# Four inner RMS norms without TensorE: sums by VectorE's 32x32 turns, the root as a power on GpSimd

## The chip, the cores and the metric

The kernel runs on one core of a Trainium2 chip. A core has TensorE (matrix products), VectorE, ScalarE and GpSimd (elementwise work of three kinds), SyncE (which here only issues loads), and 16 DMA engines. The engines run in parallel, each works through its own instructions in order, and they wait for one another by semaphores. The metric is the device time of the whole kernel in microseconds (us); weights and activations start in the chip's memory (HBM) and the output ends there.

## The reference

A decoder trunk of two layers on 256 tokens of width 1024, everything float32:

```python
def rms_norm(x, g):
    y = x * lax.rsqrt(jnp.mean(x * x, axis=-1, keepdims=True) + EPS)
    return y * g

# layer 0: x += short_conv_mixer(rms_norm(x, a_norm)); x += conv_glu_ffn(rms_norm(x, f_norm[0]))
# shared K, V from rms_norm(x, kv_norm)
# layer 1: x += moba_attention(rms_norm(x, b_norm), K, V); x += conv_glu_ffn(rms_norm(x, f_norm[1]))
# output: rms_norm(x, final_norm)

def short_conv_mixer(h, w_in, conv_w, w_out):      # w_in 1024 x 3072, conv of width 3 over tokens
    b_gate, c_gate, hx = jnp.split(h @ w_in, 3, axis=-1)
    return (b_gate * causal_dwconv(c_gate * hx, conv_w)) @ w_out

def conv_glu_ffn(h, w_up, conv_w, conv_b, w_down): # w_up 1024 x 5632, w_down 2816 x 1024
    u = causal_dwconv(h @ w_up, conv_w) + conv_b
    g, v = jnp.split(u, 2, axis=-1)
    return (jax.nn.silu(g) * v) @ w_down
```

The attention has 16 heads of 64; with 256 tokens there is one block, so it is plain causal attention with a relative position bias. K/V and the queries use the same normalized x up to their gains, so the trunk has five norms with a different sum: the mixer's, the first ConvGLU's, the one of K/V and attention, the second ConvGLU's, and the final one. The first four are called the inner norms.

## The kernel before, in words

**Layout.** Activations are kept transposed: feature on the 128 partitions, 8 tiles (k = 0 to 7) of 256 tokens along the free axis. A weight matrix is cut into units of 128 output columns: a unit "B" is 128x2048 (two groups of 128 columns, 48 matmuls of 128x256), a unit "S" is 128x1024 (24 matmuls). Each product is made of three matmuls on split operands: weight and activation are each split into a high part and a low remainder, and `mm3` (L168) issues high by high, high weight by low activation, low weight by high activation.

**Preparing a weight unit.** SyncE loads it (`rawB`, `rawS`, three buffers each), ScalarE copies it to `hi` (L91), VectorE subtracts to get `lo` (L97). The functions `hi(tag, part, parts)` and `lo(tag, part, parts)` (L102, L109) do this for the next unit in line, whole or a part of it; `lo` also issues the load of the unit three ahead. A unit's matmuls can start when its `hi` is there and need its `lo` at their third step.

**The order of the work.** The schedule is manual: each engine runs its instructions in the order in which the program emits them, and the program sprinkles `hi` and `lo` between the other work by hand. TensorE works through the units one after the other; VectorE and ScalarE prepare later units and do the elementwise work of earlier ones.

**A norm, before.** The matmuls don't wait for the norm. They run on x times the gain; the token's factor 1/rms is multiplied into the products afterwards (`u<-up,rr`, L456 in the mixer, L551 in the ConvGLUs), so `rr`, a tile that holds the 256 factors on every partition, is first wanted there. `boundary` (L304) adds the previous block's products to x, makes the high and low parts of the scaled x (ScalarE, VectorE), and the squares. `sum_squares` (L293) adds the eight squared tiles to one, in two halves. What is left is a sum over the 128 partitions for each token, and it must come back on every partition:

- `rstd_cols` (L338): four matmul records with a vector of ones give the sums as two columns of 128 tokens each (tokens on partitions); VectorE takes the inverse root by a bit trick and three Newton steps (`rsqrt`, L325, 10 small instructions), and scales the identity matrix by it, as high and low part.
- `rstd_rows` (L361 is its matmul): two matmuls of a matrix of ones (`each`) with these diagonal matrices broadcast the factors to all partitions, and ScalarE copies them to `rr` (L364).

TensorE gets these matmuls in the middle of up units whose own matmuls are ready; the mixer's and the ConvGLUs' code therefore splits units 1 and 2 and puts their k = 0 step later. The `again` tiles: `tile_0_again` (L277) makes a copy of activation tile 0 (high by ScalarE, low by VectorE), and a step with `again=True` reads that copy at k = 0. For V and K/V the copy's low part is `va[1]`.

**Around the four places.**
- Mixer: units MC[1], MB[1], MC[2] surround the norm; the first product that needs `rr` is L456, behind ScalarE's square of `rr`. The bias table of the attention (`bias_table`, GpSimd and others) is emitted before the mixer.
- ConvGLU (`ffn`): for unit i the chain is product with `rr` (L551, VectorE), conv (ScalarE L558, VectorE L397), Silu, product, then split parts for the down unit. `conv(i)` also emits the `hi` and `lo` of later units. ScalarE loads the Silu table (L594) with a dummy instruction, `first`, while TensorE does the norm's sum.
- K/V: units v0, v1, v2, then the query/key units; `v_step(1)` (L655 to L658) reads tile 0 in its sixth step, after the norm's sum. The V outputs need the factors as columns (`ycol`), the queries as rows scaled by -1/8 in reversed order.

The final norm (L948 on) already takes its root by a GpSimd power (L961) of one column.

Of the kernel before, what the change touches and what calls it, by code (L numbers as in the profile page):

```python
# [17 lines left out]
S = 256  # L18
# [19 lines left out]
def f32(ap):  # L38
    return ap.bitcast(F32)
# [3 lines left out]
def yoco_kernel(ctx: ExitStack, tc: tile.TileContext, t: dict, out: bass.AP):  # L43
# [95 lines left out]
    each = const.tile([128, 192], F32R, name="each")[:, 48:176]  # L139
# [5 lines left out]
    A.activation(each, ones, AF.Copy)  # L145
# [158 lines left out]
    def boundary(acc, x, gain, order=same, again=True):  # L304
# [11 lines left out]
        lo("B", 0, 2)  # L316
        if not again:
            lo("B", 1, 2)
        sum_squares(sq, 1, order)
        if again:  # L320
            lo("B", 1, 2)
            tile_0_again(xh, xl)
        return xh, xl, sq

    def rsqrt(ms, y, a, eng=V):  # L325

        eng.tensor_scalar(y.bitcast(I32), ms.bitcast(I32), -0.5, float(0x5F3759DF), op0=OP.mult, op1=OP.add)
        for _ in range(3):
            eng.tensor_mul(a, y, y)
            if eng is V:  # L330
                V.scalar_tensor_tensor(a, a, -0.5, ms, op0=OP.mult, op1=OP.mult)
                V.scalar_tensor_tensor(y, a, 1.5, y, op0=OP.add, op1=OP.mult)
            else:
                eng.tensor_mul(a, a, ms)
                eng.tensor_scalar(a, a, -0.5, 1.5, op0=OP.mult, op1=OP.add)
                eng.tensor_mul(y, a, y)

    def rstd_cols(sq, meanwhile=None):  # L338

        ps = psum.tile([128, 512], F32, name="misc", bufs=1)  # L340
        for c in range(2):
            PE.matmul(ps[:, c:c + 1], sq[:, 2, c * 128:(c + 1) * 128], ones[:, 0:1],
                      start=(c == 0), stop=True, skip_group_check=True)
        w = tmp.tile([128, 8], F32, name="nw")
        ms, y, a = w[:, 0:2], w[:, 2:4], w[:, 4:6]
        V.tensor_scalar(ms, ps[:, 0:2], 1.0 / D, EPS, op0=OP.mult, op1=OP.add)
        rsqrt(ms, y, a)
        if meanwhile:
            meanwhile()
        dh, dl = (tmp.tile([128, 384 + 64], F32R, name="d" + x, tag="z" + x, bufs=4)[:, 16:16 + S] for x in "hl")  # L350
        for c in range(2):
            d = slice(c * 128, c * 128 + 128)
            V.tensor_scalar(dh[:, d], ident, y[:, c:c + 1], None, op0=OP.mult)
            V.scalar_tensor_tensor(dl[:, d], ident, y[:, c:c + 1], f32(dh[:, d]), op0=OP.mult, op1=OP.subtract)
        return y, (dh, dl)

    def rstd_rows(dg, scales=(1.0,), orders=(same,)):

        ps = psum.tile([128, 512], F32, name="misc", bufs=1)
        for n in range(2):  # L360
            PE.matmul(ps[:, :S], each, dg[n], start=(n == 0), stop=(n == 1), skip_group_check=True)  # L361
        r = act.tile([128, 2, S], F32, name="rr", bufs=1)
        for n, s in enumerate(scales):
            A.activation(r[:, n, :], orders[n](ps[:, :S]), AF.Copy, scale=s)  # L364
        return r
# [34 lines left out]
    ext = bias_table()  # L400


# [37 lines left out]
    for q in range(4):  # L440
        hi("B", q, 4)
        squares(xT, sq, q)
        lo("B", q, 4)
        if q == 2:
            sum_squares(sq, 0)
    sum_squares(sq, 1)
    tile_0_again(xh, xl)
# [30 lines left out]
    up_step(MC[1], mc[1], xh, xl, 2, range(1, 8), first=1)  # L478
    MC[1].used = False

    def quarter(q):
# [61 lines left out]
    def ffn(layer, xh, xl, sq, bank=down_bank, between=None):  # L543
# [40 lines left out]
        for i in range(FJ):  # L584
            if between and i >= 20:
                between(i - 4, acc)
            if i != 2:
                ub[i] = up_bank()
# [461 lines left out]
```

## Time and profile before

| | before |
|---|---|
| runs | 567.91, 567.95, 567.37 us |
| median | 567.91 us |
| profiled execution | 567.37 us, its span 565.6 us |
| granted TensorE clock, mean | 0.998 |
| TensorE / VectorE / ScalarE / GpSimd busy | 559.0 / 473.5 / 341.4 / 9.6 us |

The span is the time from the first to the last profiled instruction; the execution's own time is a little longer. In a row of the trace the columns are: start in us from the span's start, duration in us, engine (PE = TensorE, DVE = VectorE, ACT = ScalarE, POOL = GpSimd), line of the kernel, operation, output<-inputs, shape and type of output and inputs, count, and in brackets, where it is given, the idle time before it on its engine with what ended it. A row of the view of groups has, after the count, total busy us and mean ns of one, then idle before it. A row of the view of stretches has the stretch, its length, TensorE's busy time with its count of matmuls in brackets, its busy share, the DMA share and GB/s moved.

### The profile page before, as it was taken

How to read it: one execution, taken by the hardware profiler on the slowest of the kernel's cores; microseconds unless marked ns; L12 is line 12 of the kernel's file. 1: busy time of each engine (PE TensorE's matmuls, PEld its weight loads, DVE VectorE, ACT ScalarE, POOL GpSimd, SP SyncE). 2: the span in 40 equal slices, each digit the busy share in tenths (PEclk: the TensorE clock that was granted, in tenths of full speed). 3: DMA queues.
4: the chain of work that ended last, by engine and by line, in shares of the span. 5: the costliest groups of instructions: out<-in, count | busy, mean ns of one | idle time of the engine just before them, and what ended most of it. 6: DMA issues, size and time to landing. Idle time of an engine off the chain costs nothing.

```text
span 565.6 us, 11835 instructions
## 1 busy us (share of the span) xinstructions
PE 559.0 (99%) x4908; PEld 555.4 (98%) x4908; DVE 473.5 (84%) x823; ACT 341.4 (60%) x528; POOL 9.6 (2%) x29
## 2 busy tenths in 40 slices
PE   9999999999999999999999999999999999999996
PEld 9999999999999999999999999999999999999995
DVE  6998869899877787787897999858999898889885
ACT  7765437567654565466756777656676566556444
POOL 0400000000000000000000000000000000000001
PEclk9999999999999999999999999999999999999999
DMA  8986573446556545655255555554656654553211
GB/s 292 387 303 223 192 294 113 159 147 247 194 189 224 189 161 209 224 177 196 76 212 169 192 216 219 191 184 150 224 187 220 226 184 165 213 222 114 75 38 75
DMA packets 24181, 108.48 MB, mean 192 GB/s; under 512 B 2736, under 2 KB 5440, under 8 KB 16192
## 3 DMA queue, kind: packets, MB, share of 16 engines
q1 hardware_dynamic: 23840, 107.43, 53.2%
q8 instruction: 38, 0.62, 0.5%
q10 hardware_dynamic: 288, 0.30, 0.1%
q14 instruction: 15, 0.12, 0.1%
HBM read 106.65 MB, written 1.07 MB: 190 GB/s over the span
## 4 chain that ended last, share of the span: by engine, by line
PE 98%; issue 0%; DVE 0%; ACT 0%; POOL 0%; POOLq 0%
PE up L169 20%; PE up L170 19%; PE up L171 19%; PE acc L169 7%; PE acc L170 7%; PE acc L171 7%; PE acc L202 3%; PE acc L203 3%; PE acc L200 3%; PE up L413 1%; PE up L785 1%; PE acc L655 1%; PE acc L657 1%; PE acc L658 1%; PE misc L142 1%; PE acc L710 1%
## 5 line engine op out<-in xcount | busy, mean ns | idle before, releaser
L169 PE MATMUL up<-xh,hiB 128*128 128x256 f32 x928 | 256.9, 277 | 0.0
L171 PE MATMUL up<-xh,loB 128*128 128x256 f32 x928 | 256.4, 276 | 0.0
L170 PE MATMUL up<-xl,hiB 128*128 128x256 f32 x928 | 256.3, 276 | 0.0
L169 PEld LDWEIGHTS up<-xh,hiB 128*128 128x128 f32 x928 | 174.2, 188 | 0.5 <-issue 0.3
L170 PEld LDWEIGHTS up<-xl,hiB 128*128 128x128 f32 x928 | 174.3, 188 | 0.0
L171 PEld LDWEIGHTS up<-xh,loB 128*128 128x128 f32 x928 | 174.2, 188 | 0.0
L97 DVE TENSOR_TENSOR loB<-rawB,hiB 128x2048 fp32r<-128x2048 f32 (+3 forms) x78 | 147.9, 1901 | 3.7 <-ACT hiB L91 3.5
L91 ACT ACTIVATE hiB<-rawB 128x2048 fp32r<-128x2048 f32 (+2 forms) x75 | 123.8, 1656 | 14.7 <-PE up L170 7.0
L558 ACT ACTIVATE cv<-u,pk 128x256 f32<-128x256 f32 x88 | 48.2, 595 | 69.3 <-DVE u L551 69.3
L97 DVE TENSOR_TENSOR loS<-rawS,hiS 128x1024 fp32r<-128x1024 f32 (+2 forms) x73 | 83.5, 1147 | 7.1 <-ACT hiS L91 6.8
L397 DVE SCALAR_TENSOR_TENSOR cv<-u,pk,cv 128x255 f32<-128x255 f32 x192 | 81.4, 479 | 2.7 <-ACT cv L558 1.7
L91 ACT ACTIVATE hiS<-rawS 128x1024 fp32r<-128x1024 f32 (+2 forms) x73 | 72.0, 987 | 8.9 <-PE acc L170 5.3
L171 PE MATMUL acc<-sh,loS 128*128 128x256 f32 x240 | 66.2, 276 | 0.0
L169 PE MATMUL acc<-sh,hiS 128*128 128x256 f32 x240 | 66.2, 276 | 0.0
L170 PE MATMUL acc<-sl,hiS 128*128 128x256 f32 x240 | 66.2, 276 | 0.0
L551 DVE TENSOR_TENSOR u<-up,rr 128x512 f32<-128x512 f32 x44 | 30.3, 689 | 42.5 <-PE up L171 40.6
L394 ACT ACTIVATE sh<-hid 128x256 fp32r<-128x256 f32 x52 | 21.7, 417 | 58.5 <-DVE hid L575 53.7
L170 PEld LDWEIGHTS acc<-sl,hiS 128*128 128x128 f32 x240 | 45.1, 188 | 0.0
L171 PEld LDWEIGHTS acc<-sh,loS 128*128 128x128 f32 x240 | 45.0, 188 | 0.0
L169 PEld LDWEIGHTS acc<-sh,hiS 128*128 128x128 f32 x240 | 45.0, 188 | 0.0
L200 PE MATMUL acc<-hiS,sh 128*128 128x256 f32 x154 | 42.5, 276 | 0.0
L202 PE MATMUL acc<-loS,sh 128*128 128x256 f32 x154 | 42.5, 276 | 0.0
(196 smaller groups left out, 796.0 us busy)
## 6 DMA issues: line engine op xcount, KB each, us to landing
rawB<-w_up SPq DMA_DIRECT2D x44, 1024.0 KB, 4.7
rawS<-w_dn SPq DMA_DIRECT2D x44, 512.0 KB, 3.4
rawB<-w_qk SPq DMA_DIRECT2D x8, 1024.0 KB, 4.8
rawB<-w_mc SPq DMA_DIRECT2D x6, 1024.0 KB, 7.6
rawS<-w_mo SPq DMA_DIRECT2D x8, 512.0 KB, 4.8
rawB<-w_v SPq DMA_DIRECT2D x4, 1024.0 KB, 4.8
rawS<-w_o SPq DMA_DIRECT2D x8, 512.0 KB, 4.0
rawS<-w_mb SPq DMA_DIRECT2D x7, 512.0 KB, 5.3
```

The costliest lines, as they stand in the source:

```text
L91: A.activation(self.hi[:, c], self.raw[:, c], AF.Copy)
L97: V.tensor_sub(self.lo[:, c], self.raw[:, c], f32(self.hi[:, c]))
L169: PE.matmul(o, wh, xh, start=start, stop=False, skip_group_check=True)
L170: PE.matmul(o, wh, xl, start=False, stop=False, skip_group_check=True)
L171: PE.matmul(o, wl, xh, start=False, stop=stop, skip_group_check=True)
L200: PE.matmul(o, hh[:, tok], u.hi[:, f], start=(first and (apart or d.start == 0)), stop=False, skip_group_check=True)
L202: PE.matmul(o, hh[:, tok], u.lo[:, f], start=False, stop=False, skip_group_check=True)
L203: PE.matmul(o, hl[:, tok], u.hi[:, f], start=False, stop=last, skip_group_check=True)
L394: return (h, lw), lambda: A.activation(h, src, AF.Copy), lambda: V.tensor_sub(lw, src, f32(h))
L397: V.scalar_tensor_tensor(o[:, back:], u[:, :S - back], w, o[:, back:], op0=OP.mult, op1=OP.add)
L551: V.tensor_mul(u, ub[j], rr[:, 0:1, :].to_broadcast([128, 2, S]))
L558: A.activation(o[:, half, :], u[:, half, :], AF.Identity, scale=cw[half][2], bias=par(P_FCB, c0 + half * FJ))
```

## The change

The sums over partitions, the inverse roots and the broadcast leave TensorE. Three new functions do them:

- `roots`: VectorE transposes the summed squares (128 x 256) in blocks of 32x32 (`V.transpose`) into a free part of the same tile, and reduces each block along its free axis: 8 columns on 128 partitions. Partition 32a+j now holds, in column b, the sum over the 32 rows of block row a of the token 32b+j. ScalarE makes three copies from partition groups 1 to 3 ("quadrants") to group 0; VectorE adds the four, scales by 1/D and adds EPS; GpSimd raises to the power -0.5; ScalarE copies the result from group 0 to the other three groups. Two callbacks, `early` and `late`, emit work meanwhile: low weights in three places, low activations for the queries in K/V.
- `rows`: one VectorE transpose of the factors, each read 32 times with a stride of zero, gives `rr` on all partitions.
- `root_rows` allocates `rr`.

`rsqrt`, `rstd_cols`, `rstd_rows` and the matrix `each` with its ScalarE copy at the start are gone. With no norm matmuls, units MC[1], MB[1], MC[2], MC[3], the ConvGLUs' units and the V and query units run whole, in the usual order of k but for the mixer's MC[1]; reads of the copied tile 0 are gone except in MC[1], v1, v3 and q0. `boundary` emits the whole low B unit ahead of the second half of the sums, for all three callers, and no copy of tile 0. In the mixer the bias table is emitted behind `roots`; `ext` is the table's tile.

```diff
-    each = const.tile([128, 192], F32R, name="each")[:, 48:176]
+    sums = const.tile([128, 64], F32, name="sums")
+    ycol = const.tile([128, 64], F32, name="ycol")
+    halves = const.tile([128, 64], F32, name="halves")
+    G.memset(halves, -0.5)
...
-    A.activation(each, ones, AF.Copy)
...
         sum_squares(sq, 0)
-        lo("B", 0, 2)
-        if not again:
-            lo("B", 1, 2)
+        lo("B")
         sum_squares(sq, 1, order)
-        if again:
-            lo("B", 1, 2)
-            tile_0_again(xh, xl)
         return xh, xl, sq
...
+    def roots(sq, early, late):
+
+        y = tmp.tile([128, 8], F32, name="nw")
+        t = sq[:, 3, :]
+        V.transpose(t, sq[:, 2, :])
+        V.tensor_reduce(sums[:, 0:8], t.rearrange("p (b i) -> p b i", i=32), axis=mybir.AxisListType.X, op=OP.add)
+        for a in range(1, 4):
+            A.activation(sums[0:32, 8 * a:8 * a + 8], sums[32 * a:32 * a + 32, 0:8], AF.Copy)
+        early()
+        ms = sums[0:32, 32:40]
+        V.tensor_reduce(ms, sums[0:32, 0:32].rearrange("p (a b) -> p b a", a=4), axis=mybir.AxisListType.X, op=OP.add)
+        V.tensor_scalar(ms, ms, 1.0 / D, EPS, op0=OP.mult, op1=OP.add)
+        G.tensor_tensor(y[0:32, :], ms, halves[0:32, 0:8], op=OP.pow)
+        late()
+        for a in range(1, 4):
+            A.activation(y[32 * a:32 * a + 32, :], y[0:32, :], AF.Copy)
+        return y
+
+    def rows(y, r):
+
+        V.transpose(r, y.rearrange("p (b o) -> p b o", o=1).to_broadcast([128, 8, 32]))
...
     # mixer
-    up_step(MC[1], mc[1], xh, xl, 2, range(1, 8), first=1)
+    up_step(MC[1], mc[1], xh, xl, 2, (*range(1, 7), 0, 7), first=1, again=True)
+    for q in range(3):
         hi("B", q, 4)
-        lo("B", q, 4)
-
-    _, dg = rstd_cols(sq, lambda: quarter(0))
-    for q in range(1, 4):
-        quarter(q)
+    y = roots(sq, lambda: lo("B", 0, 4), lambda: (lo("B", 1, 4), hi("B", 3, 4), lo("B", 2, 4)))
+    ext = bias_table()
+    rr = root_rows()
+    rows(y, rr[:, 0, :])
+    lo("B", 3, 4)
     hi("S")
     hi("B")
-    up_step(MC[1], mc[1], xh, xl, 2, (0,), first=1, again=True)
     mb[1] = acc_bank()
-    up_step(MB[1], mb[1], xh, xl, 1, (*range(1, 7), 0, 7), first=1)
+    up_step(MB[1], mb[1], xh, xl, 1)
     mc[2] = up_bank()
-    up_step(MC[2], mc[2], xh, xl, 2, range(0, 2))
-    rr = rstd_rows(dg)
     A.activation(rr[:, 1, :], rr[:, 0, :], AF.Square)
     lo("S")
-    up_step(MC[2], mc[2], xh, xl, 2, range(2, 8))
+    up_step(MC[2], mc[2], xh, xl, 2)
...
     # ffn
+            ub[i] = up_bank()
+            up_step(up[i], ub[i], xh, xl, 2)
             if i == 1:
-                n = 4 if layer else 3
-                up_step(up[1], ub[1], xh, xl, 2, range(1, n), first=1)
-                _, dg = rstd_cols(sq)
-                lo("S")
+                rr = root_rows()
+                y = roots(sq, lambda: lo("S"), lambda: lo("B"))
+                rows(y, rr[:, 0, :])
                 A.activation(first, ones[:, 0:1], AF.Silu)
-                up_step(up[1], ub[1], xh, xl, 2, (*range(n, 7), 0, 7), first=1, again=True)
-                n = 2 if layer else 1
-                ub[2] = up_bank()
-                up_step(up[2], ub[2], xh, xl, 2, range(1, n + 1), first=1)
-                rr = rstd_rows(dg)
                 gate(0, conv(0))
...
     # K/V and queries
-            if n == 1:
-                v_step(1, range(1, 5), 1)
-                ycol, dg = rstd_cols(sq)
-                v_step(1, (5, 0, 6, 7), 1, True)
-                oh = Heads("oh")
-            elif n == 2:
-                v_step(2, range(0, 3))
-                rr = rstd_rows(dg, (-0.125, 1.0), (rev, same))
-                v_step(2, range(3, 8))
+            v_step(n, again=n in (1, 3))
...
             if n == 0:
+                A.activation(va[0], f32(xvh[:, 0, :]), AF.Copy)
+                V.tensor_copy(va[1], f32(xvl[:, 0, :]))
                 scaled_hi(xT, P_BN, range(0, 6), xqh)
                 hi("B")
-                A.activation(va[0], f32(xvh[:, 0, :]), AF.Copy)
-                V.tensor_copy(va[1], f32(xvl[:, 0, :]))
                 scaled_hi(xT, P_BN, range(6, 8), xqh)
-                lo("B")
+                y = roots(sq, lambda: scaled_lo(xT, P_BN, range(0, 2), xqh, xql), lambda: lo("B"))
+                rr = root_rows()
+                rows(y, rr[:, 1, :])
             elif n == 1:
-                scaled_lo(xT, P_BN, range(0, 4), xqh, xql)
+                oh = Heads("oh")
                 hi("B")
-                lo("B")
+                A.activation(rr[:, 0, :], rev(rr[:, 1, :]), AF.Copy, scale=-0.125)
+                scaled_lo(xT, P_BN, range(2, 4), xqh, xql)
                 tile_0_again(xvh, xvl)
                 tile_0_again(xqh, xql)
+                lo("B")
                 scaled_lo(xT, P_BN, range(4, 8), xqh, xql)
+                for a in range(4):
+                    d = slice(32 * a, 32 * a + 32)
+                    V.tensor_copy(ycol[d, 0:2], y[d, a::4])
```

More of the change, by code (lines that the diff above doesn't have):

```diff
@@ L302, in square_tile, with boundary @@
         return act.tile([128, KT, S], F32, name="sq", tag="oh", bufs=1)
-    def boundary(acc, x, gain, order=same, again=True):
+    def boundary(acc, x, gain, order=same):
         xh, xl = parts_tiles()
@@ L315, in boundary @@
         sum_squares(sq, 0)
-        lo("B", 0, 2)
-        if not again:
-            lo("B", 1, 2)
+        lo("B")
         sum_squares(sq, 1, order)
-        if again:
-            lo("B", 1, 2)
-            tile_0_again(xh, xl)
         return xh, xl, sq
[L325 to L365, printed above, removed]
+    def roots(sq, early, late):
[14 more added lines that the diff above has]
+        return y
@@ L368, in yoco_kernel, with root_rows @@
+    def rows(y, r):
+        V.transpose(r, y.rearrange("p (b o) -> p b o", o=1).to_broadcast([128, 8, 32]))
+    def root_rows():
+        return act.tile([128, 2, S], F32, name="rr", bufs=1)
     ext_d = dram.tile([NH, 384], F32, name="ext_d")
@@ L399, in yoco_kernel @@
     nc.sync.dma_start(rb[:, :N_BUCKETS], t["rb"])
-    ext = bias_table()
     mc, mb, z = {}, {}, {}
@@ L445, in yoco_kernel @@
             sum_squares(sq, 0)
+    tile_0_again(xh, xl)
     sum_squares(sq, 1)
-    tile_0_again(xh, xl)
     hi("S")
@@ L507, in yoco_kernel @@
     mc[3] = up_bank()
-    up_step(MC[3], mc[3], xh, xl, 2, (1, 2, 3, 4, 5, 6, 0, 7), first=1, again=True)
+    up_step(MC[3], mc[3], xh, xl, 2)
     mixer_b(2, mixer_a(2, "S"))
@@ L586, in ffn @@
                 between(i - 4, acc)
-            if i != 2:
-                ub[i] = up_bank()
+            ub[i] = up_bank()
+            up_step(up[i], ub[i], xh, xl, 2)
             if i == 1:
-                n = 4 if layer else 3
-                up_step(up[1], ub[1], xh, xl, 2, range(1, n), first=1)
-                _, dg = rstd_cols(sq)
-                lo("S")
+                rr = root_rows()
+                y = roots(sq, lambda: lo("S"), lambda: lo("B"))
+                rows(y, rr[:, 0, :])
                 A.activation(first, ones[:, 0:1], AF.Silu)
-                up_step(up[1], ub[1], xh, xl, 2, (*range(n, 7), 0, 7), first=1, again=True)
-                n = 2 if layer else 1
-                ub[2] = up_bank()
-                up_step(up[2], ub[2], xh, xl, 2, range(1, n + 1), first=1)
-                rr = rstd_rows(dg)
                 gate(0, conv(0))
-            else:
-                again = i in (2, 6)
-                ks = (*range(n + 1 if i == 2 else 1, 7), 0, 7) if again else range(8)
-                up_step(up[i], ub[i], xh, xl, 2, ks, first=int(again), again=again)
             last = i == FJ - 1
@@ L633, in yoco_kernel @@
     acc = ffn(0, xh, xl, sq)
-    xvh, xvl, sq = boundary(acc, xT, P_KVN, rev, again=False)
+    xvh, xvl, sq = boundary(acc, xT, P_KVN, rev)
     xqh, xql = parts_tiles()
@@ L643, in yoco_kernel @@
     vb, qb, qs, sb, pr, pt, ps_, ob, bias = {}, {}, {}, {}, {}, {}, {}, {}, {}
-    ycol = rr = None
+    rr = None
     def v_step(n, ks=range(KT), first=0, again=False):
@@ L880, in yoco_kernel @@
                 qb[n] = up_bank()
-                if n == 0:
-                    qk_step(0, (1, 2, 0, *range(3, 8)), 1, True)
-                else:
-                    qk_step(n)
+                qk_step(n, again=n == 0)
             if n % 2:
```

6 lines of the change are left out of this document (1 added, 5 removed).

## The prediction

> **What bounds the kernel now.** I read the page first (busy shares, then the chain of waits), then TensorE's instruction counts in stretches of equal length.
>
> ```profile
> span 565.6 us, 11835 instructions
> ```
>
> ```profile
> PE 559.0 (99%) x4908; PEld 555.4 (98%) x4908; DVE 473.5 (84%) x823; ACT 341.4 (60%) x528; POOL 9.6 (2%) x29
> ```
>
> ```profile
> PE 98%; issue 0%; DVE 0%; ACT 0%; POOL 0%; POOLq 0%
> ```
>
> TensorE is busy for 99% of the span and carries 98% of the chain that ended last, so the end moves only by matmuls that go away, by a wait that TensorE gets, or by a change of its pace. VectorE, at 84%, prepares the low halves of the weights and is the next in line.
>
> ```profile
> 18.50:45.50 27.00, 27.00 (x240) 1.00 0.86 316
> 98.00:125.00 27.00, 27.00 (x239) 1.00 0.46 158
> 276.00:303.00 27.00, 27.00 (x238) 1.00 0.53 181
> 386.00:413.00 27.00, 27.00 (x239) 1.00 0.56 196
> 150.00:177.00 27.00, 27.00 (x240) 1.00 0.50 179
> ```
>
> Each row is a stretch of 27 us with TensorE's count of matmuls. The first four hold the four inner norms (mixer, first ConvGLU, K/V, second ConvGLU), the last holds none. Each norm has 6 records of its own (4 of the sum, 2 of the broadcast), so the real work is 234, 233, 232 and 233 matmuls against 240: what a norm costs TensorE is worth 6, 7, 8 and 7 matmuls.
>
> ```profile
> 100.95 0.50 PE L342 MATMUL misc<-ones,sq 128*128 128x1 f32 x4
> 101.63 0.28 PE L171 MATMUL up<-xh,loB 128*128 128x256 f32 x1
> 104.10 0.28 PE L171 MATMUL up<-xh,loB 128*128 128x256 f32 x1
> 127.67 0.28 PE L169 MATMUL up<-xh,hiB 128*128 128x256 f32 x1
> 127.90 0.28 PE L171 MATMUL up<-xh,loB 128*128 128x256 f32 x1
> ```
>
> Undisturbed, a matmul starts every 0.113 us (240 starts in 27.00 in the last row above; 127.67 to 127.90 is two steps). Behind the norm's sum it is slower: 101.63 to 104.10 is 21 matmuls, 0.1177 us each, and the usual pace comes back only after the matmuls that read the copied tile 0. That slow cadence is part of the price above, and returns as a rival.
>
> **What the change takes from TensorE.** All 24 records and the slow cadence behind them: 6, 7, 8 and 7 times 0.113 is 0.68, 0.79, 0.91 and 0.79 us, 3.17 us in all. Everything else in the change lies on other engines and costs nothing while TensorE finds its operands ready. So I follow the operands with the least to spare.
>
> **K/V: a wait that I can place.** The re-read of tile 0 moves to the first step of the second V unit.
>
> ```profile
> 277.65 2.35 DVE L97 TENSOR_TENSOR loB<-rawB,hiB 128x1024 fp32r<-128x1024 f32 x2
> 281.37 0.42 DVE L299 TENSOR_TENSOR sq<-sq 128x256 f32<-128x256 f32 x1
> 281.71 0.29 DVE L857 CAST vl<-xl 128x256 fp32r<-128x256 f32 x1
> 280.04 0.28 PE L655 MATMUL acc<-hiB,xh 128*128 128x256 f32 x1
> 280.28 0.28 PE L658 MATMUL acc<-hiB,xl 128*128 128x256 f32 x1
> ```
>
> The unit starts at 280.04, and its third matmul (280.28) reads the low part of the activations. From now on that is the copy that VectorE makes at 281.71 to 282.00. The copy keeps its place behind the low weights and the sums of squares (two halves of 2.35 us become one whole of about the same). Before, the copied tile came 24 matmuls and the norm's sum later, so nothing waited. Now TensorE waits 282.00 - 280.28 = 1.72 us; queued behind it is every later matmul. Net in this stage: 1.72 - 0.91 = +0.81 us. The new chain itself lies under the second V unit, and the next low weights and the query unit get later by as much as TensorE does.
>
> **The two ConvGLUs: the length of the new chain.** Prices, from groups by shape:
>
> ```profile
> L97 DVE TENSOR_TENSOR loB<-rawB,hiB 128x2048 fp32r<-128x2048 f32 x58 | 132.4, 2284 | 3.0 <-ACT hiB L91 2.9
> L97 DVE TENSOR_TENSOR loS<-rawS,hiS 128x1024 fp32r<-128x1024 f32 x65 | 79.1, 1220 | 7.1 <-ACT hiS L91 6.8
> L551 DVE TENSOR_TENSOR u<-up,rr 128x512 f32<-128x512 f32 x44 | 30.3, 689 | 42.5 <-PE up L171 40.6 <-ACT rr L364 1.8
> L758 DVE STREAM_TRANSPOSE late<-pr 32x128 f32<-32x128 f32 x40 | 12.2, 304 | 0.7
> L943 DVE STREAM_TRANSPOSE xt<-xres 32x512 f32<-32x512 f32 x16 | 11.2, 702 | 0.5
> L299 DVE TENSOR_TENSOR sq<-sq 128x256 f32<-128x256 f32 x4 | 1.7, 426 | 0.1
> L331 DVE SCALAR_TENSOR_TENSOR nw<-nw 128x2 f32<-128x2 f32 x12 | 1.9, 162 | 0.4
> L594 ACT ACT_TABLE_LOAD x2 | 2.6, 1283 | 0.0
> L594 ACT ACTIVATE first<-ones 128x1 f32<-128x1 f32 x2 | 0.4, 204 | 0.0
> ```
>
> ```profile
> 557.59 0.69 DVE L979 TENSOR_TENSOR y<-xt,gb 128x512 f32<-128x512 f32 x1
> 557.83 0.88 POOL L961 TENSOR_TENSOR nl<-nl 128x1 f32<-128x1 f32 x1 [290.71 <-DVE nl L960]
> 560.86 0.56 POOL L961 TENSOR_TENSOR nl<-nl 128x1 f32<-128x1 f32 x1 [2.15 <-DVE nl L960]
> ```
>
> A turn of 256 columns lies between 304 and 702 ns: 0.44 by the slope. The first reduction I take as an add of 256 columns, 0.43 (0.35 to 0.69 as bounds), the small ones 0.16 to 0.19 (L331). Dependent VectorE steps stand some 0.035 apart. A small ScalarE copy is 0.20; three in a row I take as 0.42 (bound 0.61). The power is the large unknown: for one column it takes 0.56 alone, but 0.88 with a VectorE product of two SBUF operands beside it, and it ends 0.43 after that product (558.71 against 558.28). So a VectorE instruction that got in first holds GpSimd up, and the low weights put into the wait are just such a product, started right behind the scaling. I let the power end 0.60 after them (bounds: 0.43, and eight columns each at the full price, 3.4).
>
> From T, the end of the sums of squares: turn and reduction to T+0.93; the small low weights (1.22, over ScalarE's three copies), reduction and scaling to T+2.37; the large low weights, which start some 0.08 before that, to T+4.56; power T+5.16; ScalarE's copies back T+5.63; turn T+6.11; first product T+6.83. ScalarE has the Silu table behind its copies, 1.28 + 0.20, which lay in an idle stretch before; it is free for the convolution at T+7.04, and that is what counts, since the convolution, two high halves and Silu follow on it in one queue.
>
> ```profile
> 99.90 0.42 DVE L299 TENSOR_TENSOR sq<-sq 128x256 f32<-128x256 f32 x1
> 107.89 1.10 ACT L558 ACTIVATE cv<-u,pk 128x256 f32<-128x256 f32 x2 [0.76 <-DVE u L551]
> 123.84 2.28 DVE L97 TENSOR_TENSOR loB<-rawB,hiB 128x2048 fp32r<-128x2048 f32 x1
> 386.06 0.43 DVE L299 TENSOR_TENSOR sq<-sq 128x256 f32<-128x256 f32 x1
> 393.82 1.10 ACT L558 ACTIVATE cv<-u,pk 128x256 f32<-128x256 f32 x2 [0.76 <-DVE u L551]
> 410.61 2.28 DVE L97 TENSOR_TENSOR loB<-rawB,hiB 128x2048 fp32r<-128x2048 f32 x1
> 413.15 0.28 PE L171 MATMUL up<-xh,loB 128*128 128x256 f32 x1
> ```
>
> The whole low weights ahead of the last sums, in place of a half, set T 1.06 later (2.28 less 1.22): 101.38 and 387.55. The first convolution then starts at 108.42 and 394.59, later by 0.53 and 0.77 us. VectorE and ScalarE answer each other from there to the low weights of up unit 5, without waiting for TensorE, so the delay is handed on whole. In the first ConvGLU these weights end at 126.12 and are wanted at 127.90: 1.78 less 0.53 and less TensorE's 0.79 leaves 0.46, no wait, and the gain of 0.79 stays. In the second they end at 412.89 and are wanted at 413.15: 0.26 less 0.77 less 0.79 is a wait of 1.30 us, so +0.51 net.
>
> By the Trainium skill (ScalarE: Activation LUTs, Rules for kernel authors) a switch to another table set is to be budgeted at some 2.7 us. The row above has the load at 1.28 us; by the page the chain would be 1.4 us longer and the sum +2.2 us, but the row measures this very instruction, so it decides. The Trainium skill (GPSIMD Engine Reference, Elementwise — side-by-side cycle accounting) gives 2.6 cycles an element for a two-input GpSimd loop, an estimate of 0.02 us for seven more columns; with that the power would end 0.45 after the low weights and the sum would be 0.15 lower.
>
> **The mixer.** Its first product stood at 26.73 behind ScalarE's square of the broadcast and VectorE's low weights.
>
> ```profile
> 26.73 0.41 DVE L456 TENSOR_TENSOR u<-up,rr 128x256 f32<-128x256 f32 x1
> 48.95 1.22 DVE L97 TENSOR_TENSOR loS<-rawS,hiS 128x1024 fp32r<-128x1024 f32 x1
> 50.85 0.28 PE L171 MATMUL up<-xh,loS 128*128 128x256 f32 x1
> ```
>
> Here the filling work is in quarters of a unit, so the power is held up less, and the bias table no longer runs ahead of it; I get the product at about 26.5. The tightest operand down the line ends at 50.17 and is wanted at 50.85: 0.68, just what TensorE gains. The gain of 0.68 stays, with nothing to spare.
>
> **Sum.** -0.68 - 0.79 + 0.81 + 0.51 = -0.15 us. The profiled execution took 567.37 us around its span of 565.6; it is the lowest of the three runs and 0.54 under their median, so -0.15 is 567.2 beside it and 567.8 beside the median of 567.91, which I give. Head and tail stay: the removed copy at the start lay in ScalarE's wait for data. With the low bounds the second ConvGLU's wait shrinks to some 0.9 us, with the high ones of all but the power it grows by some 0.7.
>
> **Rivals.** A difference under 0.2% (1.14 us) can't be told from none here.
> - *The power is not held up* (GpSimd gets its operands in first; the row at 557.83 speaks against it). The chain shortens by about 1.3 us, the second ConvGLU keeps 0.79: -0.68 - 0.79 + 0.81 - 0.79 = -1.45, 566.5 us. Chance 0.12.
> - *No wait at the second V unit*, if the copy gets there early: -0.15 - 1.72 = -1.87, 566.0; with no wait in the second ConvGLU either -3.17, 564.7. For it: nothing in the order of VectorE's rows; against it 281.71. Together 0.12.
> - *Slower: the slow cadence takes hold*. In the second ConvGLU TensorE restarts from a wait, as it does behind the norm's sum (100.95), and no re-read of a copied tile follows to end it. From unit 5 on 17 up units of 48 matmuls and as many down units of 24 are left, 1224; at 0.0044 more each (0.1177 for 0.1133) that is up to 5.4 us, 3.6 if only the up units are hit: 571 to 573. It decides as soon as that wait exists. Against it: other restarts may find their pace. Chance 0.16.
> - *Slower: a dear power*, 3.0 us rather than 0.60. All chains get 2.4 longer: the mixer's tight operand 1.4 late, the ConvGLUs +1.2 and +2.9: about +6, 574; it decides from 0.5 us more upwards. Chance 0.12.
>
> **Chances and range.** The forecast has 0.45, own range 566.8 to 568.7; 0.03 is for the rest. Faster: 0.24 from the rivals and 0.04 from the forecast's low edge; same 0.41; slower 0.28 and the upper edge, 0.31. The range 565.9 to 571.6 leaves out the full gain and the dear ends of the two slow cases.
>
> **What would show it.** No matmul with the sums or the broadcast; TensorE idle near 280.3 for 1.7 us until the copied low tile; the power ending just after the large low weights; idle before unit 5's first low matmul of 1.3 us in the second ConvGLU and none in the first; 0.113 us a matmul behind both waits. It is wrong if the waits are not there, if others are (the mixer's low weights, the first down units), or if the pace behind a wait is 0.118.

## The result and the profile after

The changed kernel takes 573.75 us (573.67 to 574.23, four executions) against 567.66 of the kernel before; the ratio is 1.0109 (95% interval 1.0091 to 1.0127). The forecast was 567.8 us, with no difference as the likeliest outcome, and a range of 565.9 to 571.6: the time lies outside it. The profiled execution took 573.67 us around a span of 571.5. In all ratios here, executions more than 1.5% above the fastest of the same kernel are left out; for kernels whose executions scatter, as some below do, the single times are given too.

The head of the page and the chain of waits of the changed kernel:

```profile
span 571.5 us, 11784 instructions
```

```profile
PE 76%; DVE 12%; ACT 5%; issue 3%; POOL 2%; DMA 2%; SPq 0%; POOLq 0%; ACTq 0%; DVEq 0%
```

TensorE carried 98% of the chain before and carries 76% now: VectorE, ScalarE and GpSimd have come onto the path that sets the end. TensorE's matmuls in the stretches that the prediction used, with the same columns:

```profile
18.50:45.50 27.00, 25.98 (x223) 1.00 0.84 312
98.00:125.00 27.00, 27.00 (x239) 1.00 0.46 158
150.00:177.00 27.00, 27.00 (x241) 1.00 0.57 210
276.00:303.00 27.00, 25.12 (x213) 1.00 0.44 144
386.00:413.00 27.00, 26.96 (x233) 1.00 0.52 180
```

(The 1.00 in these rows is the granted TensorE clock; where the columns were explained above, it was called a busy share by mistake.) The mixer's and the K/V stretch, which held no wait before, now have 1.0 and 1.9 us of it. The places, from TensorE's own rows (start, duration, instruction, then idle time before it and what ended it):

```profile
31.81 0.39 PE L173 MATMUL up<-xh,loB 128*128 128x256 f32 x1 [0.37 <-DVE loB L97]
41.21 0.39 PE L173 MATMUL acc<-sh,loS 128*128 128x256 f32 x1 [0.65 <-DVE loS L97]
129.32 0.39 PE L173 MATMUL up<-xh,loB 128*128 128x256 f32 x1 [0.50 <-DVE loB L97]
283.48 0.39 PE L620 MATMUL acc<-hiB,vl 128*128 128x256 f32 x1 [1.55 <-DVE vl L808]
301.05 0.39 PE L173 MATMUL up<-xh,loB 128*128 128x256 f32 x1 [0.34 <-DVE loB L97]
419.02 0.39 PE L173 MATMUL up<-xh,loB 128*128 128x256 f32 x1 [1.52 <-DVE loB L97]
```

Six waits, each for something that VectorE makes. The idle times understate them, since a matmul's modelled end is later than the start of the next one in a full pipeline: counted from start to start, less one undisturbed step of 0.1133, the six are 0.53, 0.82, 0.67, 1.71, 0.50 and 1.68 us, and the step behind each costs a further 0.11 (its "restart" below). Smaller stops stand at 52.24 (0.03 us), 400.12 (0.05) and in the first down unit of the second ConvGLU, at 405.85 and 406.33 (0.20 and 0.15).

**Where the 5.9 us are.** Both traces hold the same 4884 matmuls in the same stages (the norms' 24 left out), so the start of the n-th matmul after, less its start before, gives the loss up to there:

| stage | forecast | measured | saved (norm matmuls, slow pace behind them) | paid |
|---|---|---|---|---|
| before the mixer's norm | 0 | +0.18 | | the load of the second part of x: ScalarE got it at 7.17 for 6.23 (other profiled executions have -0.34 to +0.39 here) |
| mixer | -0.68 | +1.33 | 0.66 | waits 1.57 with their restarts, slow pace and the stop at 52.24 together 0.42 |
| first ConvGLU | -0.79 | -0.01 | 0.94 | wait 0.78, pace and restart 0.15 |
| K/V and first queries | +0.81 | +2.70 | 0.70 | waits 2.43, slow pace 0.97 |
| second ConvGLU | +0.51 | +1.74 | 0.86 | waits 2.35, slow pace 0.25 |
| sum | -0.15 | +5.94 | 3.16 | 7.13 waits, 1.79 pace |

(A wait includes its restart; the pace is what is left over.) The saving of 3.17 us that the prediction counted is there in sum; by stage it was off by up to 0.21, and that these errors cancel is luck. It is the price that was wrong.

**The new chain.** GpSimd's and VectorE's rows at the power, in the mixer, the first ConvGLU, K/V and the second ConvGLU (of each pair, VectorE's low weights, then the power beside them):

```profile
21.97 1.27 DVE L97 TENSOR_TENSOR loB<-rawB,hiB 128x512 fp32r<-128x512 f32 x2
105.20 2.29 DVE L97 TENSOR_TENSOR loB<-rawB,hiB 128x2048 fp32r<-128x2048 f32 x1
285.45 2.29 DVE L97 TENSOR_TENSOR loB<-rawB,hiB 128x2048 fp32r<-128x2048 f32 x1
394.04 2.29 DVE L97 TENSOR_TENSOR loB<-rawB,hiB 128x2048 fp32r<-128x2048 f32 x1
```

```profile
22.14 2.63 POOL L334 TENSOR_TENSOR nw<-sums,halves 32x8 f32<-32x8 f32 x1 [20.61 <-DVE sums L333]
105.36 3.66 POOL L334 TENSOR_TENSOR nw<-sums,halves 32x8 f32<-32x8 f32 x1 [72.78 <-DVE sums L333]
285.70 3.53 POOL L334 TENSOR_TENSOR nw<-sums,halves 32x8 f32<-32x8 f32 x1 [17.12 <-DVE sums L333]
394.29 3.53 POOL L334 TENSOR_TENSOR nw<-sums,halves 32x8 f32<-32x8 f32 x1 [105.05 <-DVE sums L333]
```

The power ends 1.53, 1.53, 1.49 and 1.49 us after the end of the low weights (22.14 + 2.63 = 24.77 against 21.97 + 1.27 = 23.24, and so on), whether these took 1.27 or 2.29. The forecast had 0.60 there.

### The profile page after: what moved, and what is told of

It reads as the page before. It is cut to its first block, busy times and chain, and to the rows that moved or that the text cites. A ratio compares the mean times of both kernels' runs of the same rounds, so it can differ in the third digit from the quotient of the medians.

```text
span 571.5 us, 11784 instructions
## 1 busy us (share of the span) xinstructions
PE 560.0 (98%) x4884; PEld 554.4 (97%) x4884; DVE 468.5 (82%) x782; ACT 343.7 (60%) x545; POOL 24.1 (4%) x34
## 4 chain that ended last, share of the span: by engine, by line
PE 76%; DVE 12%; ACT 5%; issue 3%; POOL 2%; DMA 2%; SPq 0%; POOLq 0%; ACTq 0%; DVEq 0%
PE up L173 15%; PE up L171 15%; PE up L172 15%; PE acc L171 5%; PE acc L173 5%; PE acc L172 5%; DVE loB L97 4%; PE acc L205 3%; PE acc L204 3%; PE acc L202 3%; POOL nw L334 2%; DMA rawB<-w_mc 2%; ACT hiB L91 1%; DVE xl L289 1%; PE up L747 1%
## 5 line engine op out<-in xcount | busy, mean ns | idle before, releaser
L97 DVE TENSOR_TENSOR loB<-rawB,hiB 128x2048 fp32r<-128x2048 f32 (+2 forms) x75 | 147.6, 1971 | 4.3 <-ACT hiB L91 4.2
L205 PE MATMUL acc<-hiS,sl 128*128 128x256 f32 x154 | 42.6, 277 | 0.0
```

What stands on the lines that cost most here:

```text
L97: V.tensor_sub(self.lo[:, c], self.raw[:, c], f32(self.hi[:, c]))
L205: PE.matmul(o, hl[:, tok], u.hi[:, f], start=False, stop=last, skip_group_check=True)
```

## The experiments

Two theories stood at the start. A: a power has a price per column and, besides, waits until a VectorE product that began first is done. B: nothing is held up, and eight columns simply cost 3.5 us. When the times of the first runs scattered by up to 16 us, a third question came in: TensorE's pace (theory P).

### The price of a power

Seven powers whose results nobody reads, in the kernel before, three at its start and four in the first ConvGLU's loop:

```diff
+    def power(i, p, n):
+        G.tensor_tensor(pw[0:p, 8 * i:8 * i + n], ones[0:p, 0:n], half[0:p, 0:n], op=OP.pow)
+
+    power(0, 32, 1)
+    power(1, 32, 8)
+    power(2, 128, 8)
...
+            if layer == 0 and i in (8, 10, 12, 14):
+                power(i // 2 - 1, 32, (1, 2, 4, 8)[i // 2 - 4])
```

> The kernel before, with seven GpSimd powers added whose results nobody reads: at the start, with VectorE still idle, of 32x1, 32x8 and 128x8; in the first ConvGLU, beside VectorE's work, of 32x1, 32x2, 32x4 and 32x8. Theory A (a power has a price for each column, and is held up as well by a VectorE product that started first): alone 0.56 us for one column and 1.5 for eight, the same on 32 and on 128 partitions; beside VectorE up to 2.3 us more, different from case to case. Theory B (no holding up, eight columns at 0.44 each): alone about 3.5 us for eight columns, and the same 3.5 in the ConvGLU. The time of the whole says nothing here beyond some tenths of a us.

567.15 us. The first two ran while VectorE was idle; VectorE's first instructions, from 4.04 on, fell into the second half of the third. The other four did not wait for the ConvGLU: nothing held them back, so they ran right behind the bias table, beside the mixer's VectorE work. GpSimd's rows, then the VectorE rows beside the last four:

```profile
1.10 0.54 POOL L148 TENSOR_TENSOR pw<-ones,half 32x1 f32<-32x1 f32 x1
1.62 1.64 POOL L148 TENSOR_TENSOR pw<-ones,half 32x8 f32<-32x8 f32 x1
3.24 1.64 POOL L148 TENSOR_TENSOR pw<-ones,half 128x8 f32<-128x8 f32 x1
27.39 2.58 POOL L148 TENSOR_TENSOR pw<-ones,half 32x1 f32<-32x1 f32 x1
29.95 0.70 POOL L148 TENSOR_TENSOR pw<-ones,half 32x2 f32<-32x2 f32 x1
30.63 1.15 POOL L148 TENSOR_TENSOR pw<-ones,half 32x4 f32<-32x4 f32 x1
31.76 2.24 POOL L148 TENSOR_TENSOR pw<-ones,half 32x8 f32<-32x8 f32 x1
```

```profile
27.27 2.28 DVE L97 TENSOR_TENSOR loB<-rawB,hiB 128x2048 fp32r<-128x2048 f32 x1
29.46 1.00 DVE L407 SCALAR_TENSOR_TENSOR cv<-u,pk,cv 128x255 f32<-128x255 f32 x2
...
31.30 1.22 DVE L97 TENSOR_TENSOR loS<-rawS,hiS 128x1024 fp32r<-128x1024 f32 x1
```

Alone, one column costs 0.54 and eight cost 1.64, on 32 or on 128 partitions alike: 0.157 us for each further column. One column issued just behind a 2.28 us product takes 2.58 and ends 0.42 after it; eight columns behind a product that ends at 32.52 end at 34.00, 1.48 after it. Theory A holds in both halves; the changed kernel's 1.5 us is the 0.43 of one column and 7 x 0.157. The 32x4 power, which was there first, took 1.15 us, and the product that began beside it at 31.30 its usual 1.22. The Trainium skill (SBUF — State Buffer, Who interferes with whom) says that a VectorE instruction with two SBUF inputs contends with a GpSimd instruction that reads SBUF. By the Trainium skill (the same section) it is the order of issue that decides which of the two is blocked. For GpSimd as the later one the rows agree; for VectorE as the later one, behind this small power, the 1.22 us show no block.

### The ConvGLUs without work behind the power

```diff
-                y = roots(sq, lambda: lo("S"), lambda: lo("B"))
+                y = roots(sq, lambda: lo("S"), lambda: None)
```

The low weights of up unit 3 then come from `conv(0)`, behind the first product.

> The changed kernel; in the two ConvGLUs nothing is put behind the power any more, the low weights of up unit 3 come behind the first product instead. Theory A: the power takes 1.5 us in the ConvGLUs in place of 3.6; VectorE's first tap comes some 0.7 us earlier counted from the end of the sums; the wait at up unit 5 goes from 0.78 to about 0.1 in the first ConvGLU and from 1.79 to about 1.1 in the second, and the waits at the first down unit there shrink; 572.0 us. Theory B: the power keeps its 3.6 us, the tap comes 1.3 us later, both waits grow by as much, 576.3 us.

```profile
106.34 1.67 POOL L334 TENSOR_TENSOR nw<-sums,halves 32x8 f32<-32x8 f32 x1 [74.28 <-DVE sums L333]
401.17 1.63 POOL L334 TENSOR_TENSOR nw<-sums,halves 32x8 f32<-32x8 f32 x1 [104.45 <-DVE sums L333]
```

The power takes its lone price, `rr` is turned 4.86 us after the first turn began in place of 6.86, the first ConvGLU has no wait left and unit 5 of the second one waits 0.49 in place of 1.68. TensorE was slow in this execution, which by itself leaves the weights more time; the run `reread` below has the same edit at the fast pace and shows the same, no wait at unit 5 of the first ConvGLU and 0.50 in the second. That is theory A by its rows. But the time was not 572.0: the executions lie between 569.58 and 585.75 us, median 575.92, ratio 1.01 (1.0064 to 1.0137), and the profiled one took 584.39. Its stretches of TensorE, on both sides of a stop in the mixer, and on into the ConvGLUs:

```profile
41.00:51.00 10.00, 10.00 (x90) 1.00 0.49 168
51.71 0.39 PE L173 MATMUL up<-xh,loS 128*128 128x256 f32 x1
52.00:62.00 10.00, 10.00 (x87) 1.00 0.64 209
56.00:83.00 27.00, 27.00 (x231) 1.00 0.69 233
150.00:177.00 27.00, 27.00 (x231) 1.00 0.54 198
440.00:467.00 27.00, 27.00 (x232) 1.00 0.54 197
```

231 matmuls where 240 or 241 were, with no wait and the granted clock at 1.00 (the counts include those that reach over an edge; 231 to 240 is as 0.1133 to 0.1177). Behind the mixer's large wait at 40.69 the pace was still the fast one. TensorE fell into the slow pace behind a stop of only 0.02 us at 51.71, at the low weights of mixer unit 4, and kept it for some 2000 matmuls, until V unit 1 waited and read a copied tile; it did so again behind the wait at unit 5 of the second ConvGLU, to the end. The operand at 51.71 is the one that the prediction found with "nothing to spare" (wanted at 50.85 in the kernel before).

### The root on VectorE

```diff
-        G.tensor_tensor(y[0:32, :], ms, halves[0:32, 0:8], op=OP.pow)
+        a, r = sums[0:32, 40:48], y[0:32, :]
+        V.tensor_scalar(r.bitcast(I32), ms.bitcast(I32), -0.5, float(0x5F3759DF), op0=OP.mult, op1=OP.add)
+        for _ in range(3):
+            V.tensor_mul(a, r, r)
+            V.scalar_tensor_tensor(a, a, -0.5, ms, op0=OP.mult, op1=OP.mult)
+            V.scalar_tensor_tensor(r, a, 1.5, r, op0=OP.add, op1=OP.mult)
```

> The changed kernel with the root taken on VectorE (the bit trick and three Newton steps, 10 small instructions on 32x8) in place of the GpSimd power, ahead of the late low weights. The root costs VectorE about 2.0 us and is done 4.3 us from the end of the sums, where the power ended at 6.1. Theory A: ScalarE's copies are then hidden under the low weights, the turn comes about 0.3 us earlier than now (6.6 for 6.9), so the four stages gain 0.3 each at most: 572.5 to 573.3 us. A theory by which the power is the whole of the loss would have it back at about 568.

The ten steps run from 106.06 to 107.91, 1.85 us, and the turn starts 6.36 us after the first one, 0.50 earlier than with the power; unit 5 of the second ConvGLU waits 1.27 in place of 1.68. The chain so moved as theory A has it. The time went the other way, 580.89 us (579.11 to 585.42; ratio 1.0262, 1.0215 to 1.031): the profiled execution (579.11) has the slow pace from the mixer's wait at 40.18 to V unit 1, 488 matmuls of the mixer and 1560 of the first ConvGLU's stage, which is 2.1 and 6.9 us at 0.0044 each. As a test of the time it says nothing on the power; it sent me to the pace.

### The wait at V unit 1

```diff
-            v_step(n, again=n in (1, 3))
+            if n == 1:
+                v_step(1, (1, 2, 3, 4, 5, 0, 6, 7), 1, True)
+            else:
+                v_step(n, again=n == 3)
```

> The changed kernel with V unit 1 in the order k = 1 to 5, 0, 6, 7, so that the copied low tile is wanted 30 matmuls later. The 1.71 us wait at 281.7 goes. Theory A (the norm's chain sets VectorE and ScalarE through the whole K/V stage, and TensorE only waits for them in another place): waits appear at V unit 2's and query unit 0's and 1's low weights, 1.5 to 1.8 us in all, and the time stays at 573.3 to 573.8 us. Theory B (the wait was a cost by itself): 571.9 us.

The wait at 283.48 is gone and others stand in its place, at the first low matmul of V unit 2 (0.64 with its restart), of query unit 0 (0.86) and of query unit 1 (1.35, it was 0.61):

```profile
295.66 0.39 PE L619 MATMUL acc<-loB,xh 128*128 128x256 f32 x1 [0.37 <-DVE loB L97]
302.09 0.39 PE L173 MATMUL up<-xh,loB 128*128 128x256 f32 x1 [0.58 <-DVE loB L97]
308.90 0.39 PE L173 MATMUL up<-xh,loB 128*128 128x256 f32 x1 [1.08 <-DVE loB L97]
```

They are the three places named, but 2.85 us in all, more than the 1.5 to 1.8 expected. From the start of V unit 1 to the first attention units the loss is 2.69 us against 2.70. The executions are 581.58, 573.08, 573.76 and 581.84 us: the lower two are those of the changed kernel, so theory A (the wait only moves, VectorE and ScalarE set the stage) holds, and not the rival's 571.9. The upper two are 8 us higher. The profiled one of them (581.58) shows the slow pace from a stop of 0.02 us at 52.09, the place of 51.71 above, to V unit 1: two paces make two groups of times.

### The pace

Three runs for it. First the kernel before, with the re-reads of the copied tile 0 in the ConvGLUs (units 1, 2 and 6) made reads of tile 0 itself:

```diff
-                up_step(up[1], ub[1], xh, xl, 2, (*range(n, 7), 0, 7), first=1, again=True)
+                up_step(up[1], ub[1], xh, xl, 2, (*range(n, 7), 0, 7), first=1)
...
-                up_step(up[i], ub[i], xh, xl, 2, ks, first=int(again), again=again)
+                up_step(up[i], ub[i], xh, xl, 2, ks, first=int(again))
```

> The kernel before, with the reads of the copied tile 0 in the two ConvGLUs (up units 1, 2 and 6) replaced by reads of tile 0 itself; order, waits and everything else as they were. Theory P (TensorE falls to 0.1177 us a matmul behind the norm's sum or behind a wait, keeps that pace, and a matmul that reads the copied tile ends it): the slow pace holds from up unit 1 to the V units in layer 0 and to the end in layer 1, some 1550 and 1500 matmuls at 0.0044 each, +6.9 and +6.6: about 581 us. Rival (the pace comes back by itself, the re-reads do nothing): 567.3 to 568.0 us.

581.05 us (580.60 to 581.37), ratio 1.0228 (1.021 to 1.0246): theory P to a tenth. Its stretches, the first one ahead of the ConvGLU's norm:

```profile
56.00:83.00 27.00, 27.00 (x240) 1.00 0.69 247
150.00:177.00 27.00, 27.00 (x232) 1.00 0.54 197
440.00:467.00 27.00, 27.00 (x232) 1.00 0.57 203
```

Then the changed kernel once more:

> The changed kernel itself, run again. Theory P: behind each of its waits TensorE goes on at one of two paces, and no re-read follows in the mixer and the ConvGLUs, so single executions may stand several us above 573.7, none far below. Rival (its waits alone set the time): all at 573.5 to 574.5.

572.88, 572.95, 581.23 and 580.80 us, median 576.88, ratio 1.0157 (1.0101 to 1.0212). The four executions behind the first result had all fallen on the lower group. The changed kernel has no single time: it has 573 or 581. That the pace behind the mixer's stops divides the two is read from the run `v1_order`; an upper execution of the changed kernel itself was not profiled.

The trace of the changed kernel's first result (573.67) shows two more things about the pace. The rows are TensorE's stretches behind its wait at 31.81, behind its wait at 41.21, in K/V behind V unit 1's wait, and, for comparison, in a quiet stretch:

```profile
32.50:40.50 8.00, 8.00 (x69) 1.00 0.72 242
42.00:50.00 8.00, 8.00 (x73) 1.00 0.41 145
284.50:300.50 16.00, 16.00 (x138) 1.00 0.55 193
56.00:72.00 16.00, 16.00 (x144) 1.00 0.61 215
```

A second wait can end the slow pace as well as a first one can begin it. And a read of a copied tile does not always end it: the K/V stretch holds such a read, the first step of query unit 0, with 0.1178 us a matmul before it and behind it, and no wait at it. Query unit 2 also still reads a copied tile (it is missing in the list of the remaining reads given with the change); there, too, the pace stays slow.

Then the kernel of the second experiment with a copied tile read again behind each place of a wait (mixer unit 5, up unit 6 of both ConvGLUs):

```diff
-        up_step(MC[j], mc[j], xh, xl, 2)
+        up_step(MC[j], mc[j], xh, xl, 2, (1, 2, 3, 4, 5, 6, 0, 7) if j == 5 else range(8), first=int(j == 5), again=j == 5)
...
-            up_step(up[i], ub[i], xh, xl, 2)
+            up_step(up[i], ub[i], xh, xl, 2, (*range(1, 7), 0, 7) if i == 6 else range(8), first=int(i == 6), again=i == 6)
...
+            if i == 3:
+                tile_0_again(xh, xl)
```

> The changed kernel with nothing put behind the power in the ConvGLUs (as in the run of that name) and with reads of a copied tile 0 put back behind the waits: in mixer unit 5, and in up unit 6 of both ConvGLUs. Theory P: the slow pace ends there in every execution; what is left is the waits, 571.0 to 572.0 us, with executions within 1 us or so of each other. Rival (the spread of 569.6 to 585.8 without the re-reads came from something else, such as the loads): the spread stays, median about 576.

570.81 us, six executions from 570.34 to 571.21, ratio 1.0049 (1.0034 to 1.0064). The scatter of 16 us is gone with three re-reads, so it was the pace and not the loads. The evidence is in the six times: in the profiled execution the pace was fast before each of the three reads, so its trace does not show them at work.

### K/V by itself

On top of the last run, and made after the runs of the next section (V unit 1 is then issued in `meanwhile`, and query unit 0 reads its copied tile as its third step):

```diff
...
-                y = roots(sq, lambda: scaled_lo(xT, P_BN, range(0, 2), xqh, xql), lambda: lo("B"))
+                def meanwhile():
+                    vb[1] = acc_bank()
+                    v_step(1, (1, 2, 3, 4, 5, 0, 6, 7), 1, True)
+                    hi("B")
+                    scaled_lo(xT, P_BN, range(0, 4), xqh, xql)
+
+                y = roots(sq, lambda: lo("B"), meanwhile)
+                tile_0_again(xvh, xvl)
+                tile_0_again(xqh, xql)
+                lo("B")
                 rr = root_rows()
                 rows(y, rr[:, 1, :])
...
-                v_out(0)
             elif n == 2:
                 hi("B")
                 lo("B")
+                v_out(0)
```

> The run reread with the K/V stage of best1 alone: the low weights of V unit 2 and query unit 0 ahead of the norm's second half, V unit 1 reading its copied tile late, the outputs of V unit 0 behind the high weights of query unit 1. By the count of K/V in the trace of the changed kernel (waits 1.82 and 0.61, slow pace 0.60 there and 0.37 in the first attention units) it gives back 3.2 to 3.4 us: 567.4 to 567.7. If the wait only moves, as in v1_order: 570.3 to 571.2.

567.36 us (566.91 to 569.31), 3.45 less than without the edit, ratio 1.0001 (0.9991 to 1.001). The reading order alone moved the wait; together with the low weights ahead of the norm's second half and the later outputs of V unit 0 it frees the stage. Which of these two does most, no run separates.

### All waits together

`best1` adds to that the Silu table inside the power (`roots`' third argument), `lo("S")` left out of the gates of units 1 and 2 so that down unit 2's low weights come behind up unit 5's, and in the mixer:

```diff
-lambda: (lo("B", 1, 4), hi("B", 3, 4), lo("B", 2, 4)))
+lambda: (lo("B", 1, 4), hi("B", 3, 4), hi("S"), lo("B", 2, 4)))
     ext = bias_table()
     rr = root_rows()
     rows(y, rr[:, 0, :])
+    A.activation(rr[:, 1, :], rr[:, 0, :], AF.Square)
     lo("B", 3, 4)
-    hi("S")
     hi("B")
...
-    A.activation(rr[:, 1, :], rr[:, 0, :], AF.Square)
```

> The changed kernel with every wait attacked: nothing behind the power in the ConvGLUs, the Silu table loaded while the power runs, the low weights of down unit 2 moved behind those of up unit 5; in the mixer ScalarE's square ahead of the next high weights; in K/V the low weights of V unit 2 and query unit 0 ahead of the norm's second half, V unit 1 reading its copied tile late, the outputs of V unit 0 behind the high weights of query unit 1; re-reads of tile 0 in mixer unit 3 and up units 6. If waits and pace are the whole loss: 567.7 less 3.2 and 0.2 for the re-reads, 564.6 to 565.6 us. If the new norm holds up something else as well (VectorE's or ScalarE's total): 567 or more.

(Its re-read in the mixer stands in unit 5, as in the run before.) 565.89 us (565.28 to 566.14, six executions), ratio 0.9961 (0.9946 to 0.9975): ahead of both kernels, and 0.3 above the range expected. Its chain, and the one wait of TensorE over 0.1 us behind the start:

```profile
PE 91%; DVE 3%; ACT 2%; issue 1%; DMA 1%; POOL 1%; SPq 0%; POOLq 0%; DVEq 0%
```

```profile
39.87 0.38 PE L173 MATMUL acc<-sh,loS 128*128 128x256 f32 x1 [0.45 <-DVE loS L97]
```

A last try took aim at this wait by low weights ahead of the taps in mixer steps 1 and 3:

```diff
         A.activation(o[:, 0, :], m[:, 0, :], AF.Identity, scale=w[2])
+        if fill == "BS":
+            hi("S")
         hi("B")
-        if fill:
-            lo(fill)
+        for tag in fill or ():
+            lo(tag)
```

> The run best1 with its last wait attacked, 0.61 us of TensorE at the first mixer-output unit's low weights (39.9 us): in mixer steps 1 and 3 the high weights of the next S unit go ahead of those of the next B unit, and its low weights ahead of the two taps. (Its re-read in the mixer stands, as in best1, in unit 5, not in unit 3 as the expectation of best1 said.) Waits as the only loss left: 565.9 less 0.7, 565.0 to 565.4 us. If VectorE, busy without a pause from 25 to 44 us, only hands the wait to mixer unit 4: 565.7 to 566.1.

566.62 us (565.90 to 567.33, and one at 576.66), ratio 0.9981 (0.9972 to 0.999). Neither of the two expected ranges held. The wait went on to the next two mixer-output units (0.64 at 42.71 and 0.36 at 54.08), so this order made no slack for VectorE there. The same kernel without the three re-reads:

> The run best2 without its three re-reads of a copied tile 0 (mixer unit 5, up unit 6 of both ConvGLUs). Theory P: with no norm on TensorE and no wait left in the mixer and the ConvGLUs there is nothing that lowers the pace, so the time is that of best2 within 0.3 us; were a wait left, executions of 568 to 572 us would appear among the others. Rival (the pace falls by itself without re-reads): all executions above 570 us.

566.12, 565.51, 565.64, 565.88 and one at 580.75 us. The median, 565.88, is 0.7 us below best2's, not within 0.3. So where waits are nearly gone the pace mostly holds by itself; in the profiled execution (566.12) the slow pace behind the mixer's wait at 43.25 ended at a stop at 54.84, with no copied tile read. The 580.75 is 15 us above the others and further off than the expected 572. It was not profiled, and neither was the 576.66 with re-reads; what happened in these two stays open.

## Why the prediction was wrong

**What held.** The gain: 3.17 us counted, 3.16 found, and the last three stages of `best1`, where hardly a wait is left, stand 0.9, 0.7 and 0.7 below the kernel before. The wait at V unit 1: 1.72 forecast, 1.71 measured, at the matmul named. The place of the ConvGLUs' largest waits (up unit 5's first low matmul). That the power is held up by the low weights in front of it.

**The mis-sized term: the power.** "I let the power end 0.60 after them (bounds: 0.43, and eight columns each at the full price, 3.4)". It ends 1.5 after them. The row for one column was read rightly (0.43), and the seven further columns were put at 0.17 in all where they cost 7 x 0.157 = 1.10. The bounds held the value, the choice between them stood too near the lower one: only one row existed, and nothing in it spoke for cheap columns. The estimate of 0.02 us for seven columns was worked out from the 2.6 cycles an element that the Trainium skill (GPSIMD Engine Reference, Elementwise — side-by-side cycle accounting) gives for a plain two-input loop. A power is another operation: the rows of the ladder give some fifty times as much, and they decide. With three copies at 0.65 for 0.42, ScalarE was free for the convolution 8.2 us after the sums and not 7.04. In the first ConvGLU that turns 0.46 of spare into the 0.67 us wait measured; in the second it makes 2.5 us out of 1.30. There 2.35 came: 1.79 at unit 5, and the rest at the first down unit (405.85 to 406.56), a place that the prediction had only among its signs of being wrong.

**The mixer: a queue that was not followed.** I put the first product at about 26.5 us; it came at 28.68. ScalarE's rows between them:

```profile
24.80 0.65 ACT L337 ACTIVATE nw<-nw 32x8 f32<-32x8 f32 x3 [2.51 <-POOL nw L334]
25.47 1.06 ACT L91 ACTIVATE hiS<-rawS 128x1024 fp32r<-128x1024 f32 x1
26.44 1.90 ACT L91 ACTIVATE hiB<-rawB 128x2048 fp32r<-128x2048 f32 x1
28.25 0.40 ACT L469 ACTIVATE rr<-rr 128x256 f32<-128x256 f32 x1
```

The copies wait for the power, two high halves are queued behind the copies, and the square that the first product needs is queued behind those. Before, high halves ran on ScalarE while TensorE and VectorE made the sums and roots. I had costed the square's operand, not its place in ScalarE's queue. The runs separate this: the mixer's stage loses 1.33 to 1.41 us in four profiled executions with this queue (the first result, `after_rep`, `reread` and `reread_kv`), and 0.21 in `best1`, where the square goes ahead and one high half runs during the power. I had also followed only the tightest operand (50.85): it waits 0.03 us, since the waits at two operands ahead of it had by then held TensorE back by 1.35.

**K/V: one wait counted, two paid.** 1.72 less 0.91 was the forecast. To it come the restart (0.11), the wait at query unit 1 (0.61: the factors' columns are copied late, V unit 0's output waits for them on ScalarE, and the next high weights stand behind that output), and 0.97 us of slow pace from the first of them on; the saving was 0.70. "The next low weights and the query unit get later by as much as TensorE does" was wrong: they hang on VectorE's and ScalarE's chain, as `v1_order` and `reread_kv` showed from both sides.

**The rivals.** The dear power (0.12, "about 574") had the right cause and the wrong size, 1.2 us a chain and not 2.4. That its total fits is luck: the rest came from places outside its sum, and other executions took 581. The slow pace (0.16, 571 to 573) is real and was under-weighted, and it came elsewhere. Behind the wait in the second ConvGLU, where the rival had it, the profiled execution went on at the fast pace. But it needs no wait there: in `v1_order`, `ffn_late` and `dve_newton` it began in the mixer, and no other stop ended it through the whole first ConvGLU. It cost the profiled execution at most 1.8 us, and others some 8. The two rivals are not alternatives; a long chain makes the waits, and behind a wait the pace can be the lower one.

## What to carry to other kernels

A serial chain of small operations that hides under a busy engine is worth what its longest price says, so measure an operation at the size in which it will run before it goes there: a one-column row says nothing of eight columns. Work put into a wait is free only if it doesn't hold up what one waits for, and if what is queued behind the waiting instruction has time; follow each queue, not the operands alone. A stop of 0.02 us can matter more than one of 1.7, by the pace that follows it. And an edit that removes "useless" re-reads or adds a wait can change the pace of what comes behind: count matmuls in a quiet stretch, and run several executions.

## What the runs showed that I had not expected

TensorE has two steady paces for the same matmuls at the same granted clock of 1.00: 240 or 241, or 231 or 232, in 27 us (0.1133 and 0.1177 us each). The slower one began behind waits (31.81 in the changed kernel), behind the norm's small matmuls (101.51 in the kernel before) and, with no stop at all, at the first matmul of V unit 1 (280.04 in the kernel before, ahead of its norm's sum). It then stayed for up to some 2000 matmuls. It ended where an operand was read from a copy at another address (104.3 in the kernel before; without these reads it stayed, `no_reread`), or behind another wait (41.21 in the changed kernel). In K/V of the changed kernel it outlasted reads of a copied tile. Why a stop sometimes lowers the pace and sometimes not, why a copied tile ends it in one place and not in another, and what happens inside TensorE, no run here tells.
